# Attention's output projection as seven block products, ahead of the plain gate products

## The chip, the core and the metric

The kernel runs on one core of a Trainium2 chip. The metric is the device time of one execution in microseconds (us); three runs were timed, and one more execution was recorded by the profiler. TensorE multiplies matrices, VectorE and ScalarE do the element-wise work, GpSimd (the profile calls it POOL) does small things and issues transfers that add into their target, and SyncE (SP) issues most other transfers.

## The reference

A hybrid encoder block in float32 on 1024 tokens of width 1024: attention and a gated recurrence run on the same normalised input, each has an output projection, and two sigmoid gates merge them. An output matrix, a squared-ReLU MLP and a final norm follow. The part that the change touches:

```
u = xn @ w_in                     # q, k, v, f, i, q_hg, g_hg, gate_sb, gate_hg
o_sb = stick_breaking_attention(...)          # (1024, 512)
o_hg = hgrn2_chunkwise(...)                   # (1024, 512), normalised, times silu(g_hg)
g_a  = sigmoid(gate_sb + b[:1024])
g_b  = sigmoid(gate_hg + b[1024:])
merged = g_a * (o_sb @ w_o_sb) + g_b * (o_hg @ w_o_hg)
h = x + merged @ w_out
```

## The kernel before

**Products.** A float32 product is made of three: each operand is split into a high part, rounded to the type that TensorE takes at full rate, and the rest, the low part (hi_lo, L164: ScalarE copies the high part, VectorE subtracts it). three (L570) issues high by high, high by low and low by high. So each operand costs a ScalarE copy and a VectorE subtraction before TensorE can use it, and each tile of 512 columns by 128 rows costs three matmuls for each 128 of depth.

**Seven products for eight.** The two gates, the output matrix and the MLP are already computed in blocks of two by two with Winograd's form of Strassen's scheme: seven products of sums of blocks in place of eight. For the gates, the two halves of the input's depth and the two gate matrices are such blocks. "Plain" gate products (raw_job, L1399) need no sum of the input: for each block of 128 columns they are 36 matmuls, p1 (first half of the depth, gate a), p4 and the gate a itself. The others (products 6, 5, 7 and 3, GatePair, L1555) need sums of the normalised input (forms).

**Streams.** TensorE's order is written out by hand in two lanes: a main lane (attention's scores, turning and values, then the recurrence's levels and tails) and a filling lane of jobs. Stream (L503) holds the jobs in order. A step of a job is mostly six matmuls; advance (L558) runs some steps between two pieces of the main lane. Starting a job splits its weights, and prefetch (L525) splits the next unit's and loads the one behind. Where a manual dependency (after, L120) is given it fixes only the order of issue.

**Order around the change.** In attention, 64 items (8 heads by 8 query blocks) are filled with projections up to the plain block KT+1 (j_att); n_fill counts the steps. Then come the recurrence's heads (h = 0 to 4, a head's levels beside the tail of the one before) filled at a fixed number of steps per piece (FILL): q2, i, f3, q3, the eight plain blocks cb = 0 to 7, then the attention's projection in four jobs sb_job (L1505), each two blocks of 128 columns by two halves of the tokens by four matmul triples. The first block of an sb job multiplies by the gate from memory, the second is copied out (yd). During the sb jobs sum_forms (L1461) makes the forms of the input's sums on VectorE, from high and low parts added in place by transfers (whole_input, L1455). Last come the gates (gates, L1751): for each block x6, y5, x7, y3, with what is left of the fourth sb job in the first of them (SB_HELD).

**Weights.** out_weight_sums (L1337) builds the output matrix's sums of blocks in DRAM, by accumulating transfers from GpSimd's queue, one in every second item of attention. The gates' weight sums are made by VectorE from the loaded blocks (RawUnit.split_t, L1384, and GatePair.split, L1589).

**Memory.** On-chip tiles come from pools: 40 tiles of 1024 columns (slots), 10 of 512 (halves), two each of raw, high and low weights, 8 PSUM banks. A tile waits until an older one is free.

Of the kernel before, what the change touches and what calls it, by code (L numbers as in the profile page):

```python
# [2 lines left out]

# [36 lines left out]
def kernel(  # L40
# [404 lines left out]
    class Unit:  # L445


        late = False
# [54 lines left out]
    class Stream:  # L503
        def __init__(self, eager=False):
            self.eager = eager
            self.jobs = []
            self.pos = 0
            self.gen = None
            self.steps = 0
            self.owed_t = None  # L510
# [703 lines left out]
    def hg_tail(h):  # L1214
# [19 lines left out]
        st.finish(j_i)  # L1234
        open_block("main")
# [72 lines left out]
    a_sb, a_hg = Split("asb"), Split("ahg")  # L1308
# [38 lines left out]

    def gate_bias(which, cb):
        return prm[:, BG + which * KT + cb : BG + which * KT + cb + 1]

    def gate_cols(which, cb):
        if cb < KT:
            c0 = (C_GA, C_GB)[which] + cb * P
        else:
            c0 = C_GH + (2 * (cb - KT) + which) * P
        return slice(c0, c0 + P)

    class RawUnit(Unit):
# [5 lines left out]
        def __init__(self, cb):  # L1364
            dmas = [
                [(0, P, W_IN[:, gate_cols(w, cb)].rearrange("(k p) c -> p k c", p=P))]
                for w in range(2)
            ]
            super().__init__(f"wga{cb}", dmas)
            if cb < KT:  # L1370
                self.roomy = (1,)

        def split(self):
            if self.hl is not None:
                return
            self.load()
            ra, rb = self.raw
            h, l = (
                wpool.tile([P, 1024], F32R, tag=t, name=f"{self.name}{t}") for t in ("whi", "wlo")
            )  # L1380
            hi_lo(h, l, ra)
            self.hl = [(h, l)]

        def split_t(self, behind=None, upto=3):  # L1384
            ra, rb = self.raw
            while self.turned < upto:
                self.turned += 1
                if self.turned == 1:
                    after(sub(rb, ra, rb), behind)
                elif self.turned == 2:  # L1390
                    after(sub(rb[:, 512:], rb[:, 512:], rb[:, 0:512]), behind)
                else:
                    t = slot(f"{self.name}t", F32R)
                    self.hl.append((t[:, 0:512], t[:, 512:]))
                    after(hi_lo(*self.hl[1], rb[:, 512:]), behind)
# [3 lines left out]
    def raw_job(cb):  # L1399
        u = raw_units[cb]  # L1400

        def steps_of(ps, wt, w0, half_, k0, start):
            wh, wl = u.hl[wt]
# [8 lines left out]

        def body():
            p1, p14, g1 = (half(f"{n}_{cb}") for n in ("p1", "p14", "g1"))
            ps, p4 = bank(f"pga{cb}"), bank(f"pgq{cb}")
            if 6 <= cb < KT:
                load_g1(cb - 6)
            if 5 <= cb < KT:
                sb_units[cb - 5].load()
            if 3 <= cb < KT - 1:  # L1420
                osb[cb - 3] = slot(f"osr{cb}")
                load(osb[cb - 3], od[cb - 3])
            yield from steps_of(ps, 0, 0, 0, 0, True)
# [5 lines left out]
            yield from steps_of(p4, 1, 0, 1, 4, True)  # L1429
            add(p14, p1, p4)  # L1430
            if cb == 3 or cb == KT - 1:
                whole_input(1, int(cb == KT - 1))
            nc.gpsimd.dma_start(pd[cb][:, 1, :], p14)
            yield from steps_of(ps, 0, 4, 0, 4, False)
            if cb < KT:
                nc.scalar.activation(g1, ps, AF.Sigmoid, bias=gate_bias(0, cb))
            else:
                nc.scalar.activation(g1, ps, AF.Sigmoid)
                mul(g1, ps, g1)
            nc.scalar.dma_start(gd[cb], g1)  # L1440
            if 4 <= cb < KT:
                a_sb.put(cb - 4, osb.pop(cb - 4))
# [3 lines left out]
    side, g1r = [], {}  # L1446
# [5 lines left out]
    forms, whole = {}, {}  # L1452
    WAIT = 7

    def whole_input(i, j):  # L1455
        for kp in range(2):
            h, l = (t.bitcast(F32) for t in xn.t[i, 2 * j + kp])
            nc.gpsimd.dma_start(l, h, accum_op=ALU.add)
            whole[i, j, kp] = l

    def sum_forms():  # L1461


        raw = whole
        def split(m, kp, src):
            forms[m, kp] = tuple(slot(f"gs{n}{m}{kp}", F32R) for n in "hl")
            hi_lo(*forms[m, kp], src)

        for j in range(2):
            whole_input(0, j)  # L1470
        yield from range(WAIT)
        s1, s2 = {}, {}
        for kp in range(2):
            s1[kp] = slot(f"gs1{kp}")
            ins = add(s1[kp], raw[1, 0, kp], raw[1, 1, kp])
            if kp == 0:
                after(ins, hg_sum[0])
            yield
        for kp in range(2):
            split(5, kp, s1[kp])  # L1480
            yield
        for kp in range(2):
            s2[kp] = slot(f"gs2{kp}")
            sub(s2[kp], s1[kp], raw[0, 0, kp])
            yield
            split(6, kp, s2[kp])
            yield
        gates_in[0].load()
        gates_in[0].load_sums()
        for kp in range(2):  # L1490
            s3 = slot(f"gs3{kp}")
            sub(s3, raw[0, 0, kp], raw[1, 0, kp])
            split(7, kp, s3)
            yield
        gates_in[0].split()
        for kp in range(2):
            s4 = slot(f"gs4{kp}")
            sub(s4, raw[0, 1, kp], s2[kp])
            split(3, kp, s4)
            yield  # L1500
        gates_in[1].load()

    sb_units = []

    def sb_job(cp):  # L1505
        src = W_OSB[:, cp * 256 : (cp + 1) * 256].rearrange("(k p) c -> p k c", p=P)
        unit = Unit(f"wo0{cp}", [[(0, 256, src)]])
        unit.roomy = (0,)
        sb_units.append(unit)

        def body():
            if cp == 0:
                side.append(sum_forms())
            for j in range(2):
                cb = 2 * cp + j
                if 1 < cb + 1 < KT:
                    load_g1(cb + 1)
                g1 = g1r[cb]
                for i, cs in halves():
                    ps = bank(f"pys{cb}_{i}")  # L1520
                    for _ in proj_half(
                        ps, unit.hl[0], a_sb.mov, 4, i, lambda k: k * 256 + j * P
                    ):
                        next(side[0], None)
                        yield
                    if i == 0:
                        mul(g1, ps, g1)
                        nc.gpsimd.dma_start(yd[cb][:, i, :], g1)
                    else:
                        y = half(f"ys{cb}")  # L1530
                        nc.scalar.copy(y, ps)
                        nc.scalar.dma_start(yd[cb][:, i, :], y)

        return st.add([unit], body)
# [12 lines left out]
    j_att = raw_job(KT + 1)  # L1547
# [4 lines left out]
    j_raw = [raw_job(cb) for cb in range(KT)]  # L1552
    j_sb = [sb_job(cp) for cp in range(4)]

    class GatePair:  # L1555
# [3 lines left out]
        def load(self):  # L1559
            cb = self.cb  # L1560
            self.raw = [
                wpool.tile([P, 1024], F32, tag="raw", name=f"wg{cb}r{i}") for i in range(2)
# [26 lines left out]
        def split(self, behind=None):  # L1589
# [4 lines left out]
            after(sub(r0[:, s0], r0[:, s1], r0[:, s0]), first)  # L1594
            sub(r1[:, s0], r1[:, s1], r0[:, s0])
# [8 lines left out]
            sub(r0[:, s1], r1[:, s1], r0[:, s1])  # L1604
# [33 lines left out]
        def gated(self, which, first, second):  # L1638
# [11 lines left out]
            if which == 0:  # L1650
                muls()
# [16 lines left out]
        def x7(self):  # L1668
            self.product(7, self.X, False)
            p1, p14 = self.p[:, 0:512], self.p[:, 512:1024]  # L1670
            self.y_sum = add(p1, p1, self.Y)
            add(p1, p1, self.X)
# [15 lines left out]
        def y3(self):  # L1688
            self.product(3, self.Y, False)
            add(self.u2, self.u2, self.Y)  # L1690
# [52 lines left out]
    SB_HELD = {KT: 4}  # L1743
# [7 lines left out]
    def gates():  # L1751
        for v, n, m in zip(gates_in, gates_in[1:] + [None], gates_in[2:] + [None] * 2):
# [8 lines left out]
            st.advance(SB_HELD.get(v.cb, 0), j_sb[3])  # L1761
# [4 lines left out]
            st.finish(j_sb[3])  # L1766
# [629 lines left out]
    n_fill = 9 * (NHS - 1 + 5) + 10  # L2396
    n_first = 4
    ready = deque()
    wsums = out_weight_sums()
    done = 0  # L2400
    for i, it in enumerate(items):
# [52 lines left out]
    st.finish(j_sb[2])  # L2454
    for _ in side[0]:
# [100 lines left out]
```

## Time and profile before

| | |
|---|---|
| median of three runs | 1419.71 us (1419.6 to 1419.95) |
| the profiled execution | 1420.01 us |
| its span in the trace | 1418.2 us |
| TensorE busy | 1408.0 us, 6848 matmuls |
| VectorE busy | 1049.5 us |
| ScalarE busy | 659.3 us |
| GpSimd busy | 145.0 us |
| traffic | 241.91 MB, mean 171 GB/s |

A row of instruction groups has the source line (often a helper's), the engine, the operation, output and inputs by the program's names, how many, busy us, mean ns of one, and the idle time of the engine just ahead of them with what ended it. The chain of waits is followed back from the last instruction, at each step to what released it. The stretches give each engine's busy time between two moments, counted from the span's start.

### The profile page before, as it was taken

How to read it: one execution, taken by the hardware profiler on the slowest of the kernel's cores; microseconds unless marked ns; L12 is line 12 of the kernel's file. 1: busy time of each engine (PE TensorE's matmuls, PEld its weight loads, DVE VectorE, ACT ScalarE, POOL GpSimd, SP SyncE). 2: the span in 40 equal slices, each digit the busy share in tenths (PEclk: the TensorE clock that was granted, in tenths of full speed). 3: DMA queues.
4: the chain of work that ended last, by engine and by line, in shares of the span. 5: the costliest groups of instructions: out<-in, count | busy, mean ns of one | idle time of the engine just before them, and what ended most of it. 6: DMA issues, size and time to landing. Idle time of an engine off the chain costs nothing.

```text
span 1418.2 us, 18602 instructions
## 1 busy us (share of the span) xinstructions
PE 1408.0 (99%) x6848; PEld 1183.5 (83%) x6848; DVE 1049.5 (74%) x1429; ACT 659.3 (46%) x1127; POOL 145.0 (10%) x282
## 2 busy tenths in 40 slices
PE   9999999999999999999999999999999999999998
PEld 7888888888888888888888888888888888888886
DVE  6667777778567888887788897676766657668765
ACT  6455555554243554433244764445444443534343
POOL 3011223110011031000000300000000000000042
PEclk9999999999999999999999999999999999999999
DMA  8344445435135685364585514444446974776725
GB/s 253 83 119 127 104 101 102 104 77 154 60 75 169 224 223 186 120 214 156 162 298 194 186 53 170 163 163 142 138 145 239 351 269 148 278 274 242 273 97 186
DMA packets 169730, 241.91 MB, mean 171 GB/s; under 512 B 30844, under 2 KB 97960, under 8 KB 169640
## 3 DMA queue, kind: packets, MB, share of 16 engines
q1 hardware_dynamic: 151432, 192.48, 41.0%
q0 software_dynamic: 11616, 34.61, 9.9%
q10 hardware_dynamic: 6592, 13.63, 2.7%
q8 instruction: 54, 0.88, 0.3%
q14 instruction: 36, 0.29, 0.1%
HBM read 170.43 MB, written 68.16 MB: 168 GB/s over the span
## 4 chain that ended last, share of the span: by engine, by line
PE 97%; ACT 1%; DMA 1%; DVE 1%; issue 0%; POOL 0%; SPq 0%; POOLq 0%; DVEq 0%; ACTq 0%
PE pm L128 21%; PE pX L128 9%; PE pW L128 6%; PE pY L128 6%; PE pjqk L128 6%; PE pga L128 4%; PE gX L128 4%; PE gY L128 4%; PE pjf L128 3%; PE pjq L128 3%; PE pys L128 3%; PE pji L128 3%; PE pyh L128 3%; PE po L128 3%; PE z L128 2%; PE pwX L128 2%
## 5 line engine op out<-in xcount | busy, mean ns | idle before, releaser
L854 DVE TENSOR_TENSOR_SCAN rm<-rm,bits 128x512 f32<-128x512 f32 (+6 forms) x72 | 87.5, 1222 | 30.5 <-ACT rm L835 29.0
L156 ACT CAST whid<-w 128x1024 fp32r<-128x1024 f32 x30 | 31.6, 1054 | 153.8 <-PE pm L128 85.4
L128 PE MATMUL pm<-wlod,sh 128*128 128x512 f32 x240 | 93.6, 390 | 0.0
L128 PE MATMUL pm<-whid,sl 128*128 128x512 f32 x240 | 93.5, 389 | 0.0
L128 PE MATMUL pm<-whid,sh 128*128 128x512 f32 x240 | 93.4, 389 | 0.0
L128 PE MATMUL pm<-tl,sh 128*128 128x512 f32 (+1 forms) x210 | 81.3, 387 | 0.0
L128 PE MATMUL pm<-th,sl 128*128 128x512 f32 (+1 forms) x210 | 81.3, 387 | 0.0
L128 PE MATMUL pm<-th,sh 128*128 128x512 f32 (+1 forms) x210 | 81.3, 387 | 0.0
L161 DVE TENSOR_TENSOR wlod<-w,whid 128x1024 fp32r<-128x1024 f32 x30 | 36.7, 1222 | 55.0 <-ACT whid L156 54.8
L156 ACT CAST wTh<-pw 128x512 fp32r<-128x512 f32 (+2 forms) x96 | 43.7, 482 | 62.4 <-PE pw L131 60.8
L161 DVE TENSOR_TENSOR wTl<-pw,wTh 128x512 fp32r<-128x512 f32 (+2 forms) x96 | 50.5, 548 | 28.9 <-ACT wTh L156 28.6
L161 DVE TENSOR_TENSOR sl<-sa,sh 128x1024 fp32r<-128x1024 f32 x56 | 68.2, 1218 | 0.6 <-ACT sh L156 0.6
L2173 POOL TENSOR_SCALAR fss<-fss 128x1 f32<-128x1 f32 x8 | 4.3, 543 | 562.0 <-ACT fsc L2168 561.5
L156 ACT CAST sh<-sa 128x1024 fp32r<-128x1024 f32 x56 | 57.2, 1045 | 7.8 <-DMA sa<-ad 7.8
L128 PEld LDWEIGHTS pm<-wlod,sh 128*128 128x128 f32 x240 | 45.1, 188 | 9.9 <-DVE wlod L161 0.4
L128 PEld LDWEIGHTS pm<-whid,sh 128*128 128x128 f32 x240 | 45.0, 188 | 9.4
L128 PEld LDWEIGHTS pm<-whid,sl 128*128 128x128 f32 x240 | 45.1, 188 | 9.2
L128 PE MATMUL pX<-sqh,t1l 128*128 128x512 f32 x128 | 50.0, 390 | 0.0
L128 PE MATMUL pX<-sql,t1h 128*128 128x512 f32 x128 | 50.0, 390 | 0.0
L128 PE MATMUL pX<-sqh,t1h 128*128 128x512 f32 x128 | 49.8, 389 | 0.0
L128 PEld LDWEIGHTS pm<-th,sh 128*128 128x128 f32 x210 | 39.5, 188 | 8.1
L128 PEld LDWEIGHTS pm<-tl,sh 128*128 128x128 f32 x210 | 39.4, 188 | 8.0
(936 smaller groups left out, 4358.8 us busy)
## 6 DMA issues: line engine op xcount, KB each, us to landing
w<-in_w_ff_dram SPq DMA_DIRECT2D x72, 512.0 KB, 4.8
sa<-ad SPq DMA_DIRECT2D x52, 512.0 KB, 6.8
ad<-a SPq DMA_DIRECT2D x32, 256.0 KB, 4.5
ad<-s SPq DMA_DIRECT2D x16, 512.0 KB, 3.2
tw<-in_w_out_dram POOLq DMA_DIRECT2D x24, 256.0 KB, 5.8
pr<-pd SPq DMA_DIRECT2D x10, 512.0 KB, 5.8
x<-in_x_dram SPq DMA_DIRECT2D x8, 512.0 KB, 7.9
xnl<-xnh POOLq DMA_DIRECT2D x8, 512.0 KB, 6.2
```

Of the source, the lines that this page charges most:

```text
L128: return pe(nc.tensor.matmul(*a, **k))
L156: hi_last[0] = after(in_turn("act", nc.scalar.copy(dst, src)), hi_behind[0])
L161: nc.vector.tensor_tensor(out=dst, in0=src, in1=hi.bitcast(F32), op=ALU.subtract),
L854: sc = nc.vector.tensor_tensor_scan(out=rr, data0=rr, data1=bits[:, 1024 - nk + a : 1024 - nk + b][:, ::-1], initial=rm[:, b : b + 1] if i ...
L2173: nc.gpsimd.tensor_scalar(out=ssq, in0=ssq, scalar1=1.0 / D, scalar2=EPS, op0=ALU.mult, op1=ALU.add)
```

## The change

Five things change.

1. **The projection** is one product of 2 x 2 blocks (halves of the tokens, halves of the depth, halves of the columns) in seven products of 256 deep by 512 by 512 each, in two jobs: products 5 and 2, then 1, 6, 7, 4 and 3. Sums of the weights are made in DRAM by accumulating transfers during attention (sb_weight_sums), sums of the attention's output by VectorE (sb_sums, sb_sums_late), and partial results are kept in tiles and banks and combined as the products end.
2. **Order.** These two jobs run ahead of the eight plain blocks, which now run in the order 0, 4, 1, 5, 2, 6, 3, 7. The plain block KT+1 moves out of attention to the place behind q3, so attention has 7 steps less to fill. A plain block now multiplies its gate by the projection loaded from memory (y0). For the last four blocks the last of three products is held back and runs in the first two gates (held_job).
3. **The gates' weight sums** are of the opposite sign and come from DRAM for the plain blocks (tg4, gate_weight_sums): VectorE's two differences for each block go, and half of the second weight load.
4. **The input's sums** are made by VectorE during attention (input_sums) and stored in DRAM; sum_forms only loads and splits them. The in-place additions by transfers go.
5. **Issue order.** The forms of the projection's operands are issued behind the copy that ends a product (hi_behind), and a step of a job also advances a side list (side).

The diff, cut to its core:

```diff
@@ Stream
+                if us[-1].alone:
+                    break
...
+            next(self.side, None)
@@ hg_tail, head 0
+        if h == 0:
+            st.side = sb_sums()
@@ weight sums of the gates
+    def gate_weight_sums():
+        for op, i, c0 in (
+            (ALU.bypass, 0, C_GA), (ALU.add, 0, C_GB), (ALU.add, 1, C_GA), (ALU.add, 1, C_GB),
+        ):
+            for r in range(4):
+                rs = slice(r * P, (r + 1) * P)
+                src = W_IN[i * 512 + r * P : i * 512 + (r + 1) * P, c0 : c0 + D]
+                after(nc.gpsimd.dma_start(tg4[rs], src, accum_op=op), scored[0])
+                yield
@@ plain blocks
+    RAW_ORDER = (0, 4, 1, 5, 2, 6, 3, 7)
+    HELD = RAW_ORDER[4:]
...
+            if cb in HELD:
+                held.append((cb, last(ps, u.kept, 0)))
             else:
+                yield from last(ps, u.hl[0], 4)
@@ the input's sums
+        for kp in range(2):
...
+            s = slot(f"xs{kp}")
+            step(s, h00, h10, ALU.subtract)
+            yield
+            step(s, s, l00, ALU.add)
+            yield
+            step(s, s, l10, ALU.subtract)
+            stored(7, kp, s)
...
+            step(s, s, h11, ALU.add)
...
+            step(s4, s, h01, ALU.add)
+            yield
+            step(s4, s4, l01, ALU.add)
+            stored(3, kp, s4)
+            yield
+            step(s, s, h00, ALU.add)
+            yield
+            step(s, s, l00, ALU.add)
+            stored(5, kp, s)
@@ their forms
+            if i < 3:
+                fetch(i + 1)
+            elif i == 4:
+                while st.pos < j_raw[-1]:
+                    yield
+                for j in range(4, 8):
+                    fetch(j)
+                gates_in[1].load()
@@ the projection
+    SB_ORDER = (5, 2, 1, 6, 7, 4, 3)
...
+        def product(m, cp):
+            open_block("fill")
+            (wh, wl), (sh, sl) = sb_w[m], sb_s[m]
+            if m in (2, 5, 1, 3):
+                sb_bank[cp] = bank(f"pys{m}{cp}")
+            ps = sb_bank[cp]
+            for k in range(2):
+                c = k * 512 + cp * P
+                ks = slice(k * 512, (k + 1) * 512)
+                three(
+                    ps, wh[:, c : c + P], wl[:, c : c + P], sh[:, ks], sl[:, ks],
+                    m in (2, 5, 1, 3) and k == 0, k == 1, True,
+                )
+            return ps
...
+            for m in ms:
+                n = SB_ORDER.index(m)
+                ahead = SB_ORDER[n + 1 : n + 3]
+                for cp in range(4):
+                    end(m, cp, product(m, cp))
+                    if cp == 0 and ahead:
+                        sb_split(ahead[0])
+                        if len(ahead) > 1:
+                            sb_load(ahead[1])
+                    if cp == 0:
+                        hi_after = sb_last[0]
+                    if cp == 1 and ahead:
+                        hi_behind[0] = hi_after
+                        sb_form(ahead[0])
+                        hi_behind[0] = None
+                    if m == 2 and cp > 1:
+                        sb_sums_late((6, 3)[cp - 2])
...
@@ the jobs
-    j_att = raw_job(KT + 1)
+    j_att = j_f[2]
...
-    j_raw = [raw_job(cb) for cb in range(KT)]
-    j_sb = [sb_job(cp) for cp in range(4)]
+    raw_job(KT + 1)
+    j_sb = [sb_job(ms) for ms in ((5, 2), (1, 6, 7, 4, 3))]
+    j_raw = [raw_job(cb) for cb in RAW_ORDER]
+    j_held = held_job()
...
-    SB_HELD = {KT: 4}
+    SB_HELD = {KT: 4, KT + 1: 5}
@@ the driver
-    n_fill = 9 * (NHS - 1 + 5) + 10
+    n_fill = 9 * (NHS - 1 + 5) + 3
-        if i % 2 == 1:
+        if i % 16 != 0:
             next(wsums, None)
+        if i > 2 and i % 5 > 1:
+            next(insums, None)
...
-        upto = (j_i, j_raw[1], j_raw[6], j_sb[1], j_sb[2])[h]
+        upto = (j_i, j_sb[0], j_raw[1], j_raw[6], j_held)[h]
```

More of the change, by code (lines that the diff above doesn't have):

```diff
@@ L2 @@
 from contextlib import ExitStack
+from itertools import chain
 import concourse.bass as bass
@@ L445 @@
     class Unit:
-        late = False
+        late = alone = False
         roomy = ()
@@ L1411, in steps_of, with last @@
                     yield
+        def last(ps, hl, w0):
+            yield from steps_of(ps, hl, w0, 0, 4, False)
+            g1 = half(f"g1_{cb}")
+            if cb < KT:
+                nc.scalar.activation(g1, ps, AF.Sigmoid, bias=gate_bias(0, cb))
+                mul(g1, g1, y0.pop(cb))
+                nc.gpsimd.dma_start(yd[cb][:, 0, :], g1)
+            else:
+                nc.scalar.activation(g1, ps, AF.Sigmoid)
+                mul(g1, ps, g1)
+                nc.scalar.dma_start(gd[cb], g1)
         def body():
-            p1, p14, g1 = (half(f"{n}_{cb}") for n in ("p1", "p14", "g1"))
+            p1, p14 = (half(f"{n}_{cb}") for n in ("p1", "p14"))
             ps, p4 = bank(f"pga{cb}"), bank(f"pgq{cb}")
[L1416 to L1423, printed above, removed]
+            if cb < KT and cb not in HELD:
+                load_y0(cb)
+            if cb == HELD[0]:
+                st.side = sum_forms()
+            yield from steps_of(ps, u.hl[0], 0, 0, 0, True)
             hi_behind[0] = nc.scalar.copy(p1, ps)
@@ L1503 @@
[L1503 to L1509, printed above, removed]
-        def body():
[L1512 to L1534, printed above, removed]
+    forms = {}
@@ new lines, in sb_load, with sb_split @@
+    def sb_load(m):
+        plain = {1: (0, 0), 2: (1, 0), 3: (1, 1)}
+        sums = {5: 1, 7: 3, 6: 2, 4: 4}
+        src = sb_block(*plain[m]) if m in plain else tv[sums[m]]
+        sb_raw[m] = wpool.tile([P, 1024], F32, tag="raw", name=f"wo{m}r")
+        load(
+            sb_raw[m].rearrange("p (k c) -> p k c", k=2),
+            src.rearrange("(k p) c -> p k c", p=P),
+        )
+    def sb_split(m):
+        sb_w[m] = tuple(
+            wpool.tile([P, 1024], F32R, tag=t, name=f"wo{m}{t}") for t in ("whi", "wlo")
+        )
+        hi_lo(*sb_w[m], sb_raw.pop(m))
@@ new lines, in sb_form, with sb_sums @@
+    def sb_form(m):
+        h, l = sb_s[m] = tuple(slot(f"as{n}{m}", F32R) for n in "hl")
+        if m == 5:
+            hi_lo(h, l, sb_sum[m])
+            return
+        first, c0 = {1: (0, 0), 6: (0, 0), 7: (0, 512), 2: (2, 0), 3: (2, 0), 4: (2, 512)}[m]
+        for kk in range(2):
+            cs = slice(kk * 512, (kk + 1) * 512)
+            hi_lo(h[:, cs], l[:, cs], osb[first + kk][:, c0 : c0 + 512])
+    def sb_sums():
+        for pair in range(4):
+            osb[pair] = slot(f"osr{pair}")
+            load(osb[pair], od[pair])
+            yield
+        yield
+        l, r = (cs for _, cs in halves())
+        rows_ = [(cs, osb[kk], osb[2 + kk]) for kk, cs in halves()]
+        sb_sum[5] = slot("as5")
+        for cs, a, b in rows_:
+            sub(sb_sum[5][:, cs], a[:, r], b[:, r])
+            yield
+        for cs, a, b in rows_:
+            sub(a[:, r], a[:, l], a[:, r])
+            yield
+        sb_form(5)
+        yield
@@ L1561, in load @@
             self.raw = [
-                wpool.tile([P, 1024], F32, tag="raw", name=f"wg{cb}r{i}") for i in range(2)
+                slot(f"wg{cb}r{i}")
+                if self is gates_in[0]
+                else wpool.tile([P, 1024], F32, tag="raw", name=f"wg{cb}r{i}")
+                for i in range(2)
             ]
```

237 lines of the change are left out of this document (166 added, 71 removed).

## The prediction

> **What bounds the kernel now.** I read the page first, then the stretches of the run, then the chain of waits, and last the vector engine's own order of instructions. The page and the stretches (busy us, and behind the x the number of instructions, of TensorE, weight loads, VectorE, ScalarE, GpSimd; then granted clock, DMA share, GB/s):
>
> ```profile
> span 1418.2 us, 18602 instructions
> PE 1408.0 (99%) x6848; PEld 1183.5 (83%) x6848; DVE 1049.5 (74%) x1429; ACT 659.3 (46%) x1127; POOL 145.0 (10%) x282
> 92.00:215.00 123.00, 123.00 (x714) 106.91 (x713) 91.24 (x117) 69.38 (x159) 28.66 (x74) 1.00 0.48 112
> 215.00:322.00 107.00, 107.00 (x618) 92.86 (x618) 77.24 (x101) 62.28 (x142) 21.18 (x50) 1.00 0.48 94
> 322.00:420.00 98.00, 98.00 (x513) 83.67 (x513) 66.92 (x120) 36.34 (x78) 5.86 (x8) 1.00 0.31 91
> 420.00:477.00 57.00, 57.00 (x305) 48.52 (x304) 41.97 (x71) 25.02 (x56) 5.56 (x9) 1.00 0.64 194
> 477.00:532.00 55.00, 55.00 (x297) 46.91 (x296) 49.31 (x75) 27.31 (x56) 12.17 (x17) 1.00 0.79 216
> 555.00:577.00 22.00, 22.00 (x98) 18.21 (x97) 16.73 (x24) 8.73 (x12) 1.08 (x2) 1.00 0.60 204
> 860.00:1100.00 240.00, 240.00 (x1060) 198.81 (x1059) 165.31 (x228) 113.95 (x165) 0.00 (x0) 1.00 0.48 165
> ```
>
> TensorE is busy in every microsecond of the stretches that the change touches (attention until about 322, the recurrence with its filling until 555, the gates behind it), at full clock. A busy TensorE can still hide gaps, since one matmul is listed longer than the next one waits, so the pace must be read as well. The chain of waits (start, us, work):
>
> ```profile
> 511.99 2.77 PE pys L128 x12
> 514.76 0.89 PE sl L128 x8
> 515.65 4.10 PE pys L128 x18
> ...
> 554.93 2.75 PE gX L128 x12
> 557.68 2.72 PE gY L128 x12
> 560.40 5.44 PE pys L128 x24
> 565.84 2.72 PE gX L128 x12
> 568.56 5.44 PE pys L128 x24
> 574.00 2.72 PE gY L128 x12
> ```
>
> Piece follows piece without a gap, at 5.44/24 = 0.227 us for a 512-wide matmul, the same as 240/1060 = 0.226 where nothing but such matmuls runs. So TensorE is the bound here, and a matmul taken away is worth 0.227 us as long as no other engine comes late. The one with least left is VectorE: 49.31 of 55 us between 477 and 532.
>
> **The change, part by part.**
>
> *Matmuls.* The attention's projection is now 8 column blocks x 2 halves x 4 k x 3 = 192 matmuls (the pys of the chain). Afterwards it is 7 products x 4 column blocks x 2 k x 3 = 168, of the same 512 columns. The gate products keep their counts: 36 for each plain block, twelve of which go into the gates for four of the blocks. That is 24 fewer: 24 x 0.227 = **-5.44 us**. Moving the product KT+1 behind q3 moves its 36 matmuls (8.2 us) out of attention and changes no count.
>
> *VectorE.* What an instruction takes up is the distance of starts in a full queue, not its listed length (start, us, instruction):
>
> ```profile
> 478.04 0.68 DVE L1314 TENSOR_TENSOR p<-p,pgq 128x512 f32<-128x512 f32 x1
> 478.63 1.22 DVE L161 TENSOR_TENSOR asbl<-osr,asbh 128x1024 fp32r<-128x1024 f32 x1
> 479.77 0.68 DVE L169 TENSOR_TENSOR sl_x<-k,q 128x512 f32<-128x512 f32 x1
> ```
>
> So 0.60 us for 512 columns (listed 0.68) and 1.14 for 1024 (listed 1.22). Removed between 322 and 577: the two weight differences of eight plain blocks (8 x 1.74 = 13.9), the eight sums of the input (9.1), and of the old projection eight products with the gate, four weight and four input splits (13.9): 36.9. Added: seven weight splits (8.0), the forms (1.14 + 12 x 0.60 = 8.3), eight half sums of the attention (4.8), sixteen ends of products (9.6), eight products with the gate (4.8), and KT+1's own five steps (4.7): 40.2. In all +3.3 us in 255 us of which 193 are taken; that lies beside TensorE. What matters is where it bunches.
>
> *The tight place* is the four product groups 2, 1, 6 and 7 inside head 2 of the recurrence. Each has 4 steps of 6 matmuls (5.44 us) and needs of VectorE one weight split, two form splits, and four ends or late sums: 1.14 + 6 x 0.60 = 4.74 us. What the head itself asks for comes from the stretch 420 to 477, whose filling was plain blocks:
>
> ```profile
> 420.00:477.00 57.00, 30.20 (x120) 22.03 (x120) 0.00 (x0) 5.70 (x9) 1.00 0.64 194
> ...
> 420.00:477.00 57.00, 15.19 (x60) 10.97 (x60) 2.73 (x4) 1.00 0.64 194
> ```
>
> These are that stretch's pga and pgq alone: 180 matmuls, 30 steps or 5 blocks, each with 1.74 + 1.14 + 0.60 + 0.60 = 4.08 us of VectorE, so 20.4 of the 41.97; the head's own part is 21.6. Per four steps that is 57 x 4/30 = 7.6 us of time and 2.9 us of the head's VectorE. A new group then asks for 4.74 + 2.9 = 7.64 us in 7.6: full, not over. By listed lengths it is 1.22 + 6 x 0.68 + 2.9 = 8.2, or 0.6 us too much for each of four groups, 2.4 us. Bounds 0 to 2.4. The nearest row is a stretch where VectorE is full already, and another in attention where it nearly is:
>
> ```profile
> 97.00:112.00 15.00, 15.00 (x84) 12.83 (x83) 13.36 (x18) 8.33 (x20) 3.27 (x9) 1.00 0.56 121
> 475.00:496.00 21.00, 21.00 (x116) 18.06 (x115) 21.00 (x35) 9.08 (x16) 1.08 (x2) 1.00 0.63 200
> ```
>
> For 21 us VectorE never rests, and TensorE doesn't stop. So I take **+1.0**, below the middle.
>
> *Attention.* input_sums brings 18 vector instructions of 1024 columns, 18 x 1.14 = 20.5 us, in three of five items from the fourth on. They need 20 calls, so about 33 items, the stretch 92 to 215 (37 scans, nine for eight items):
>
> ```profile
> L854 DVE TENSOR_TENSOR_SCAN rm<-rm,bits 128x512 f32<-128x512 f32 (+6 forms) x37 | 44.5, 1213 | 9.4 <-ACT rm L835 9.3
> L161 DVE TENSOR_TENSOR wTl<-pw,wTh 128x512 fp32r<-128x512 f32 (+3 forms) x49 | 25.5, 544 | 16.9 <-ACT wTh L156 16.8
> ```
>
> VectorE has 123 - 91.24 = 31.8 us free there. The filling due (n_fill) falls from 118 to 111 steps over 64 items, so 33 items lose about 3.6 steps, some 4.2 us with the empty last step of a block left out. VectorE goes to 111.7 of 118.8 us: 94%. The new instruction is put in order behind the last low half (turn_lo), just where the engine now waits 16.8 us for ScalarE's wTh, and a scan is issued an item (3.7 us) before its transposes. Behind a late one stand this item's low half and the next scan; TensorE's values wait for them an item later. Between 0 and 20.5 us; I take **0**, since the gaps lie in the right place and the total fits.
>
> *GpSimd and the queues.* The queue gets 24 more accumulating weight transfers and eight stores of sums in attention, and loses eight in-place sums of the input later.
>
> ```profile
> L1345 POOL DMA_DIRECT2D tw<-in_w_out_dram x24 | 17.6, 764 | 0.0
> L1345 POOL DMA_DIRECT2D tw<-tw x8 | 8.5, 1302 | 0.0
> ```
>
> At most 32 x 1.3 = 42 us on an engine busy 28.66 + 21.18 of 230 us; the head's QH and QL moves and the memsets of wT stand behind them by one issue, against an item of 3.7 us. SP loses half of each second weight load and the g1 loads, and gets the eight sums (512 KB each), seven projection weights for four, and the y0 loads; DMA share is 0.48 in attention. **0**, and never below it; if the cover were gone, one issue (1.3 us) for each of a few items.
>
> *Entry of the gates.* The sums for products 7 and 3 are loaded only when the last plain block ends. x7 follows after x6, y5 and four filling steps, 2.72 + 2.72 + 5.44 = 10.9 us, as now; y3 follows at 13.6 instead of 19.0, since four steps went to KT+1.
>
> ```profile
> sa<-ad SPq DMA_DIRECT2D x52, 512.0 KB, 6.8
> hb<-hd SPq DMA_DIRECT2D x8, 512.0 KB, 9.1
> L156 ACT CAST gsh<-gs x8: 1046/1052/1072, 519.4 to 556.3; 128x1024 fp32r<-128x1024 f32 x8
> L161 DVE TENSOR_TENSOR gsl<-gs,gsh x8: 1216/1221/1226, 520.5 to 557.4; 128x1024 fp32r<-128x1024 f32 x8
> ```
>
> A load of this size takes 6.8 us, two casts 2.3: ready at 9.1, 1.8 us early. With the slow load (9.1) and VectorE full, 0.5 late, and the second and third tiles a cast later each: 0.5 + 2 x 1.2 = 2.9 us. Bounds 0 to 2.9; I take **0**, the nearer row being the 52 loads.
>
> *Sum.* The profiled execution took 1420.01 us, 1.8 more than its span: 1420.01 - 5.44 + 1.0 = 1415.6. It lay 0.3 above the median of the three runs (1419.71), so the forecast is **1415.3**.
>
> **The rivals.**
>
> *VectorE takes the saving back in the projection.* 2.4 us by listed lengths, and at each of four hand-overs one 512-wide low half not ready (0.60): 4.8 us on 1414.3, so 1419.1. For it: forms are made only two or three steps ahead, where whole units were split a job ahead. Against: the full stretch from 475 on costs nothing.
>
> *The gates wait for their sums*: 1414.3 + 2.9 = 1417.2, and with a weight split ahead of the cast (1.14) 1418.3.
>
> *Attention stretches: slower.* VectorE keeps order, and 9.3 + 16.8 = 26.1 of its 31.8 free us are waits for ScalarE. If these can't be filled, only 5.7 are free and 14.8 of the 20.5 us push TensorE: 1414.3 + 14.8 = 1429.1; with half of the 20.5 it is 1424.5. It decides from 8.3 us on (5.44 saved, 2.84 to be seen). For it: runs of three sums in a row where the queue is already nearly full (13.36 of 15 us, 97 to 112). Against: the order named above.
>
> *TensorE isn't the limit.* Weight loads fill 83%, and if the other 17% were room, 24 matmuls would fill room: 1419.7. Against: 198.81/240 is also 83% where the pace can't be had faster. The Trainium skill, Perfetto Trace Analysis, section on identifying the most-contended engine, has it that weight-load share, not matmul busy time, tells the headroom. By that rule the gain would be nothing; this trace, with 0.226 us in stretches of nothing but matmuls, shows 83% as the full pace.
>
> **How the numbers follow.** Forecast 0.62 (1413.3 to 1416.8; below the sum, since removed and neighbouring pieces run at 2.77 for 12 rather than 2.72 in places, worth up to a microsecond); VectorE in the projection 0.12; gates 0.08; attention 0.15; not the limit 0.03. This kernel's measurement can tell 0.2%, 2.84 us, from no change. Faster is 0.62, same 0.12 + 0.08 + 0.03 = 0.23, slower 0.15. The range 1413.3 to 1421.0 holds all but most of the attention case and the tail of the rest.
>
> **What would show it.** Right: 6824 TensorE instructions; the projection's pieces at 5.44 for 24, running on into the recurrence's without a gap; attention some 8 us shorter, the recurrence some 3 longer; VectorE near 94% between 92 and 211. Wrong: VectorE or ScalarE in the chain between wT and the values; sh of a projection form as what a matmul waits for; a gap ahead of KT's gX on product 7. The forecast falls if the pieces behind 92 us lose more than 2.6 us to gaps.

## The result and the profile after

The changed kernel took 1427.55 us (median of 4 runs, 1427.22 to 1428.73) against 1419.83 for the kernel before on the same chip: a ratio of 1.0056, with a 95% interval of 1.0038 to 1.0073. It is slower by 7.7 us. The forecast was 1415.3, and the range ended at 1421.0.

The profiled execution after took 1427.22 us. From its page: the span, the busy time of the engines with the number of instructions, and the shares of the chain of waits, below them the same shares of the kernel before.

```profile
span 1425.4 us, 18660 instructions
PE 1406.0 (99%) x6824; PEld 1179.2 (83%) x6824; DVE 1066.6 (75%) x1463; ACT 668.1 (47%) x1147; POOL 166.4 (12%) x318
PE 91%; DVE 4%; ACT 2%; DMA 1%; issue 1%; POOL 0%; SPq 0%; ACTq 0%; POOLq 0%; DVEq 0%
...
PE 97%; ACT 1%; DMA 1%; DVE 1%; issue 0%; POOL 0%; SPq 0%; POOLq 0%; DVEq 0%; ACTq 0%
```

The 24 matmuls are gone (6848 to 6824). Yet the span grew by 7.2 us, from 1418.2. The share of TensorE in the chain falls from 97% to 91%; VectorE's rises from 1% to 4% and ScalarE's from 1% to 2%. The stretches show where (columns as in the prediction):

```profile
92.00:215.00 123.00, 121.20 (x708) 105.07 (x708) 108.67 (x134) 69.61 (x161) 43.39 (x91) 1.00 0.77 172
215.00:314.00 99.00, 97.98 (x562) 84.51 (x561) 70.47 (x94) 56.68 (x131) 28.70 (x61) 1.00 0.81 182
...
420.00:577.00 157.00, 152.84 (x800) 128.62 (x799) 118.87 (x196) 77.44 (x165) 22.01 (x37) 1.00 0.58 190
577.00:720.00 143.00, 141.49 (x625) 116.88 (x624) 120.22 (x174) 53.18 (x69) 10.29 (x19) 1.00 0.52 175
```

The same stretches of the kernel before, three of them:

```profile
215.00:314.00 99.00, 99.00 (x573) 85.98 (x573) 71.90 (x93) 56.72 (x132) 21.18 (x50) 1.00 0.49 93
...
420.00:577.00 157.00, 157.00 (x826) 133.52 (x825) 126.41 (x193) 73.16 (x151) 24.46 (x35) 1.00 0.67 199
577.00:720.00 143.00, 143.00 (x632) 118.48 (x631) 118.36 (x169) 50.02 (x66) 9.16 (x17) 1.00 0.53 172
```

TensorE was never idle there. It now rests for 1.80, 1.02, 4.16 and 1.51 us, 8.5 us in all. A pause hidden under a matmul's listed length (0.39 us, where the next one starts after 0.227) does not show as rest. Read by the distance of starts beyond the usual one (0.227 us for 512 columns), the pauses between 95 and 725 us add up to 12.0 us: 4.8 in attention, 5.5 in the recurrence, 1.7 at the entry of the gates. Before, no single one in that stretch was above 0.14. With 5.44 saved this makes +6.6 us; the last matmul starts 5.7 us later than before (1417.2 against 1411.5 us), so the reading of the pauses is about 1 us too high.

The rest of the 7.2 us lies behind the last matmul. From its start to the end of the span it took 6.7 us before and 8.3 after; after the last output is computed, 3.5 and 5.1. At the program's end each engine has an instruction DRAIN, and GpSimd's is the one that grew. Its three, before and after (ns shortest/median/longest, first and last start in us):

```profile
L2551 POOLq DRAIN  x3: 46/102/2516, 1413.1 to 1417.9; - x3
...
L2768 POOLq DRAIN  x3: 50/93/5819, 1418.8 to 1425.1; - x3
```

The long one grew from 2.52 to 5.82 us, and in the change it ends 0.8 us before the span does. This is no pause of TensorE; the account below comes back to it.

VectorE and ScalarE don't look like the cause by their load: in the worst stretch, 420 to 577, VectorE is busy for *less* than before (118.87 against 126.41), and ScalarE for 77.44 of 157. That points to order, not load, as what stops TensorE. Three places show how. In attention, from the chain of waits after (start, us, work):

```profile
202.42 0.69 DVE wTl L162
203.11 1.13 DVE xs L1522
...
205.03 1.13 DVE xs L1522
...
207.84 0.69 DVE KS L162
...
208.55 0.68 DVE QL L162
209.23 1.13 DVE wqk7l L162
210.36 0.61 DVE wTl L162
...
211.02 1.10 PE po L129 x7
```

TensorE's values (po) wait for the low half wTl; ahead of it in VectorE's queue stand two of the new input sums (xs), two scans (rm), the head's halves KS and QL, and a weight split.

In the recurrence, from the order in time after (start, us, engine, instruction; in brackets the idle time ahead and what ended it):

```profile
515.94 0.40 PE L129 MATMUL pga<-xnh,wga1wlo 128*128 128x512 f32 x1
516.38 0.69 ACT L1460 ACTIVATE g<-pga,prm 128x512 f32<-128x512 f32 x1 [0.71 <-PE pga L129]
516.96 0.61 ACT L1097 COPY ksl<-k 128x512 f32<-128x512 f32 x1
517.62 1.05 PE L129 MATMUL sl<-q,ksl 128*128 128x128 f32 x7 [1.28 <-ACT ksl L1097]
```

The next level's matmuls (sl) need ScalarE's copy of the keys, ksl. It stands behind a sigmoid g that waits for the gate product issued just ahead. So the copy can't start before TensorE has run empty: 1.28 us.

At the entry of the gates, from the chain of waits after:

```profile
584.94 1.14 DVE ahgl L162
...
586.60 1.22 DVE wlog L162
...
588.42 1.14 DVE tgl L162
589.55 0.61 DVE pr L1324
...
590.21 1.88 PE gY L129 x7
```

Here VectorE works without a break from 576.5 us on, and gY waits for pr, which stands 13 us into this row of work.

### The profile page after: what moved, and what is told of

Its sections match the earlier page's. It is cut to its first block, busy times and chain, and to the rows that moved or that the text cites. A ratio compares the mean times of both kernels' runs of the same rounds, so it can differ in the third digit from the quotient of the medians.

```text
span 1425.4 us, 18660 instructions
## 1 busy us (share of the span) xinstructions
PE 1406.0 (99%) x6824; PEld 1179.2 (83%) x6824; DVE 1066.6 (75%) x1463; ACT 668.1 (47%) x1147; POOL 166.4 (12%) x318
## 4 chain that ended last, share of the span: by engine, by line
PE 91%; DVE 4%; ACT 2%; DMA 1%; issue 1%; POOL 0%; SPq 0%; ACTq 0%; POOLq 0%; DVEq 0%
PE pm L129 21%; PE pX L129 9%; PE pW L129 6%; PE pY L129 6%; PE pjqk L129 6%; PE gY L129 3%; PE pji L129 3%; PE pga L129 3%; PE pyh L129 3%; PE gX L129 3%; PE pjq L129 3%; PE pjf L129 3%; PE po L129 3%; PE pwX L129 2%; PE pjv L129 2%; PE z L129 2%
## 5 line engine op out<-in xcount | busy, mean ns | idle before, releaser
L157 ACT CAST wTh<-pw 128x128 fp32r<-128x128 f32 (+3 forms) x96 | 43.8, 481 | 56.3 <-PE pw L132 51.6
L129 PEld LDWEIGHTS pm<-th,sl 128*128 128x128 f32 x210 | 39.5, 188 | 8.0
```

Of the source, the lines that this page charges most:

```text
L129: return pe(nc.tensor.matmul(*a, **k))
L157: hi_last[0] = after(in_turn("act", nc.scalar.copy(dst, src)), hi_behind[0])
```

## Experiments

Two theories. **P (place):** moving KT+1 out of attention, priced at nothing in the prediction, costs most of the loss. **S (sums):** VectorE's new input sums in attention cost most, as in the third rival. The table has all runs; the time before was 1419.71 to 1419.83 in each comparison.

| kernel | median us | ratio to before, 95% |
|---|---|---|
| the change | 1427.55 | 1.0056 (1.0038 to 1.0073) |
| change, KT+1 back in attention | 1422.3 | 1.0018 (1.0009 to 1.0028) |
| change, without most input sums | 1426.11 | 1.0046 (1.0031 to 1.0061) |
| change, ksl earlier | 1422.43 | 1.0017 (1.0008 to 1.0027) |
| change, KT+1 back, ksl earlier | 1417.57 | 0.9986 (0.9976 to 0.9995) |
| the same, sums spread | 1415.93 | 0.9973 (0.9963 to 0.9983) |
| change, ksl earlier, sums spread | 1420.58 | 1.0006 (0.9997 to 1.0016) |
| change, held products' y0 earlier | 1427.48 | 1.0056 (1.0041 to 1.0071) |
| before, KT+1 moved | 1425.35 | 1.0039 (1.0024 to 1.0053) |
| before, with input sums | 1420.28 | 1.0004 (0.9995 to 1.0014) |
| before, seven steps fewer in attention | 1422.2 | 1.0018 (1.0009 to 1.0027) |
| before, ksl earlier | 1419.37 | 0.9997 (0.9987 to 1.0007) |
| before, KT+1 moved, ksl earlier | 1424.04 | 1.0033 (1.0021 to 1.0045) |

### KT+1 put back into the changed kernel

```diff
-    j_att = j_f[2]
+    j_att = raw_job(KT + 1)
...
     q_job(3)
-    raw_job(KT + 1)
...
-    n_fill = 9 * (NHS - 1 + 5) + 3
+    n_fill = 9 * (NHS - 1 + 5) + 10
```

> The changed kernel with one edit: the plain block KT+1 runs at the end of attention again, with the 7 filling steps that the old kernel had there. The changed kernel took 1427.5 us and the old one 1419.8. Theory P (moving that block is what costs: it shifts which weight cast stands in ScalarE's queue ahead of a wT cast in attention, and it puts the block's end, where ScalarE issues a store that waits for VectorE, into the recurrence): the gaps of TensorE at 223 and 269 us and those at 437 and 446 us go, about 5 us, so 1422 to 1423. Theory S (the input's sums on VectorE are what costs in attention, and the projection's own copies what costs in the recurrence): no more than 1 us better, 1426.5 to 1428.

1422.3 us: 5.2 us back. The pauses behind 200 us in attention are gone, and so is that of the gates; the one at 167 us (1.07) and 5.2 us in the recurrence stay.

### The same block moved in the old kernel

The same edit the other way round: j_att = j_f[2], raw_job(KT + 1) behind q_job(3), n_fill with + 3.

> The kernel before with one edit: the plain block KT+1 is moved out of attention to the place behind q3, and attention has 7 filling steps less. Theory P: this alone opens gaps of TensorE in attention and in the recurrence, 2 to 5 us, so 1422 to 1425. Theory S: VectorE has room in attention without the sums, and the old plain blocks follow as they did; 1419.5 to 1420.5.

1425.35 us, a little over theory P's range: the move alone costs the old kernel 5.6 us, with none of the other edits. Its pauses lie at 208, 222 and 268 us, as in the changed kernel, and in the recurrence at 515 to 523 us (2.2 and 0.9 us).

### The input's sums, taken out and put in

In the changed kernel 14 of the 18 vector instructions are left out, the loads and stores stay:

```diff
         def step(out, a, b, op):
-            after(nc.vector.tensor_tensor(out=out, in0=a, in1=b, op=op), turn_lo[0])
+            if out is not a:
+                after(nc.vector.tensor_tensor(out=out, in0=a, in1=b, op=op), turn_lo[0])
...
-            after(
-                nc.vector.scalar_tensor_tensor(
...
```

> The changed kernel, with 14 of the 18 vector instructions that form the input's sums during attention left out (what is stored is the first difference of each tile, so the sums are incomplete); stores, loads and all else stay. Theory S: the gaps of TensorE at 168 us (1.2 us) and 210 us (1.0 us), whose chain runs through these instructions, go, and some of the others in attention with them: 1424 to 1425.5. Theory P: these gaps come with the shifted filling and stay, so 1427 to 1428.

In the old kernel all 18 and their eight stores are added, their results unused:

```diff
+    insums = input_sums()
...
+        if i > 2 and i % 5 > 1:
+            next(insums, None)
```

> The kernel before with one addition: the changed kernel's 18 vector instructions for the input's sums and the eight stores of them, in the same items of attention; nothing reads what they store. Theory S: about 2.4 us of gaps between 92 and 215 us, as the changed kernel has there, so 1421.5 to 1423. Theory P: with the old filling there is room for them, 1419.5 to 1420.5.

1426.11 us, 1.4 less than the change, between the two expectations; and 1420.28, 0.6 more than before, within the measurement's uncertainty. The pause at 168 us goes without the sums, the one at 210 falls from 1.01 to 0.63; the rest stays. So the sums are a small part of the loss, and S falls as its main cause.

### Pacing alone

What does the move do in attention, where it only takes work away? In the old kernel only the number of steps due is changed; the block stays where it is and its last steps run behind the last item.

```diff
-    n_fill = 9 * (NHS - 1 + 5) + 10
+    n_fill = 9 * (NHS - 1 + 5) + 3
```

> The kernel before with one number changed: attention fills 7 steps less slowly spread over its 64 items (n_fill as in the changed kernel), and the block KT+1 stays where it was, its steps now running together after the last item. No instruction is added, removed or moved past another job. Theory P, in its sharper form (what hurts in attention is that each job's end, and with it the next weight cast, meets another item): the gaps of TensorE at 208, 222, 268 us that the moved block opened in the kernel before, 2.5 us in all, come back, 1421.5 to 1423. Against it: less filling as such does no harm, 1419.5 to 1420.5.

1422.2 us: +2.4 us, with the same pauses at 208, 222 and 268 us. From its order in time:

```profile
220.73 1.05 ACT L156 CAST wf0h<-wf0r 128x1024 fp32r<-128x1024 f32 x1 [1.85 <-PE pjqk L128]
221.69 0.75 ACT L156 CAST wTh<-pw 128x512 fp32r<-128x512 f32 x2
...
222.30 0.89 DVE L161 TENSOR_TENSOR wTl<-pw,wTh 128x512 fp32r<-128x512 f32 x2 [2.10 <-ACT wTh L156]
222.31 0.39 PE L128 MATMUL po<-wTh,V 128*128 128x256 f32 x1 [0.17 <-ACT wTh L156]
...
223.04 0.39 PE L128 MATMUL po<-wTl,V 128*128 128x256 f32 x1 [0.34 <-DVE wTl L161]
```

The next unit's weights need a buffer that the product before (pjqk) frees. Their cast (wf0h) stands in ScalarE's queue and waits 1.85 us for that product's end. Behind it stands the urgent cast wTh, and the values po wait for it and for wTl. In the kernel before, unchanged, the same casts come with no wait named:

```profile
220.78 0.57 ACT L156 CAST QH<-pjqk 64x512 fp32r<-64x512 f32 x1
221.24 1.05 ACT L156 CAST wf0h<-wf0r 128x1024 fp32r<-128x1024 f32 x1
222.19 0.47 ACT L156 CAST wTh<-pw 128x384 fp32r<-128x384 f32 x1
```

There the product had ended earlier in the item. The pauses at 208 and 268 us were not followed back in the same way. Seven steps fewer over 64 items shift the end of each job against the items, and at this hand-over the cast now comes ahead of a product's end.

### The keys' copy ahead of the sigmoid

The recurrence's pauses showed ksl behind other work of ScalarE. Here ksl is issued after the first filling step behind a level, not directly ahead of the next level's matmuls; no instruction is added.

```diff
+            if l < 6:
+                keys_due.append(lambda l=l: copy_keys(f"sl{h}_{l + 1}", 2 << l))
...
-                    st.advance(int(owed), upto)
+                    first = min(int(owed), 1)
+                    st.advance(first, upto)
+                    while keys_due:
+                        keys_due.pop()()
+                    st.advance(int(owed) - first, upto)
```

> The changed kernel with one edit in the recurrence: ScalarE's copy of the keys (ksl) for the next level is put in its queue after the first filling step behind a level, and no longer right ahead of the level's matmuls. Theory Q (in the recurrence TensorE stands because ksl waits in ScalarE's order behind a copy or sigmoid that needs the end of the product just issued, or behind a cast that nobody waits for): the gaps at 437, 446 and 515 us, 4.0 of the 5.5 us there, go: 1423 to 1424.5. Theory V (VectorE is too full there and makes the key itself late): ScalarE only waits at another place, 1426.5 to 1428.

1422.43 us: 5.1 us back, a little more than theory Q's range. From the order in time of this run, at the same level:

```profile
508.36 0.62 ACT L1103 COPY ksl<-k 128x512 f32<-128x512 f32 x1
...
513.03 1.05 PE L129 MATMUL sl<-q,ksl 128*128 128x128 f32 x8
513.23 0.69 ACT L1474 ACTIVATE g<-pga,prm 128x512 f32<-128x512 f32 x1 [0.70 <-PE pga L129]
```

The copy is done 4 us ahead of sl, and no wait stands beside sl; the sigmoid still waits for its product, but nothing urgent is behind it. The control is the same edit in the old kernel:

> The kernel before with the earlier copy of the keys alone: the control for the gain of 10 us that this edit and the block KT+1 put back brought on the changed kernel. The old kernel shows no gap of TensorE ahead of a level's matmuls, so theory Q expects nothing: 1419.3 to 1420.3. If the edit were a gain of its own, not a repair of the new order, 1414 to 1418.

1419.37 us, no difference: the old kernel's order paid nothing here. So the wait came with the new order; it wasn't there to be gained.

And in the old kernel with KT+1 moved:

> The kernel before with the block KT+1 moved (1425.4 alone) and the earlier copy of the keys. Theory Q: the gaps of 2.2 and 0.9 us ahead of a level's matmuls, which moving the block opened in the recurrence, close, and those in attention (2.6 us) stay: 1421.8 to 1422.8, what the pace alone costs (1422.2). If the moved block costs by its own vector work in the recurrence, it stays near 1425.

1424.04 us, 1.3 less than with the move alone, and a miss for theory Q, which had 1421.8 to 1422.8. The move alone, without the ksl edit, has two pauses in its recurrence, at two queues. First, from the order in time:

```profile
515.56 1.04 ACT L156 CAST wo01h<-wo01r 128x1024 fp32r<-128x1024 f32 x1 [0.46 <-PE pga L128]
516.51 0.68 ACT L1436 ACTIVATE g<-pga,prm 128x512 f32<-128x512 f32 x1
517.09 0.61 ACT L1092 COPY ksl<-k 128x512 f32<-128x512 f32 x1
...
517.75 1.16 PE L128 MATMUL sl<-q,ksl 128*128 128x128 f32 x8 [1.99 <-ACT ksl L1092]
```

This is the wait of the changed kernel: ksl stands behind a weight cast and the sigmoid. So the move alone opens it in the old kernel too, without the new projection. Then, from the chain of waits:

```profile
511.28 8.49 DMA xnl<-xnh
...
519.86 0.09 DVE gs L1314
...
521.00 1.22 DVE wo01l L161
...
523.05 0.61 DVE q L169
...
523.79 1.13 PE sl L128 x8
```

VectorE's queue is held by gs, which waits for the old kernel's in-place addition by a transfer (8.49 us); k and q of the recurrence stand behind it. The ksl edit closes the first pause (2.2 us), but TensorE then comes to the second place earlier and waits there for 2.4 us instead of 0.9. The change removes these additions, so its own recurrence doesn't have this second wait.

### Put together

> Both: the block KT+1 back in attention (1422.3 us alone) and the copy of the keys earlier. Theory Q: of the 5.2 us of gaps left in the recurrence the four ahead of a level's matmuls go, 4.0 us: 1418 to 1419, a little under the 1419.7 of the old kernel. Theory V: 1422 to 1423.

1417.57 us, a little better than theory Q's range. Then the input's sums are spread, one in every third item rather than three in a row of five:

```diff
-        if i > 2 and i % 5 > 1:
+        if i > 2 and i % 3 == 0:
             next(insums, None)
```

> As the one before, and the input's sums spread over all of attention: one vector instruction in every third item, and not three in five items of the first half. If these sums still cost there (the gap of 1.07 us at 167 us), about 1 us better than the one before; if not, the same within 0.5 us.

1415.93 us, 3.9 us under the kernel before (0.9973, 0.9963 to 0.9983), and 1.6 better than without the spreading: this version beats both. Its page and stretches:

```profile
span 1413.7 us, 18694 instructions
PE 1402.5 (99%) x6824; PEld 1179.3 (83%) x6824; DVE 1067.0 (75%) x1463; ACT 668.3 (47%) x1147; POOL 162.0 (11%) x318
```

```profile
92.00:215.00 123.00, 123.00 (x714) 106.87 (x713) 101.86 (x128) 69.39 (x159) 42.60 (x89) 1.00 0.74 160
...
420.00:577.00 157.00, 156.99 (x827) 133.69 (x826) 127.51 (x211) 82.35 (x171) 24.92 (x40) 1.00 0.60 198
577.00:720.00 143.00, 143.00 (x632) 118.25 (x631) 120.47 (x172) 51.82 (x67) 9.72 (x18) 1.00 0.54 182
```

With the same matmuls and nearly the same number of instructions in all, TensorE rests for no more than 0.01 us in these stretches. Since it doesn't stop, VectorE and ScalarE get through *more* between 420 and 577 than in the change (127.51 and 82.35 against 118.87 and 77.44), without holding it up. Last, the same with the block moved as the change has it:

> The changed kernel with the block KT+1 left where the change puts it, the earlier copy of the keys (1422.4 alone) and the input's sums spread over all of attention. The sums' share (gaps at 168 and 210 us) goes, about 1.6 us as with the block put back; the gaps of the pace (222 and 268 us), the two at 530 and 547 us and the one in the gates at 583 us stay: 1420.3 to 1421.5. The distance to the version with the block put back, 1415.9, is then what the move costs when all else is mended, about 5 us.

1420.58 us. The distance to 1415.93, 4.65 us, is the price of the move alone where all else is mended.

### The gates' pause

It was thought that gY's helper pr waits for y0, the loaded projection of a held block, so y0 was loaded at the block's start.

```diff
-            if cb < KT and cb not in HELD:
+            if cb < KT:
                 load_y0(cb)
```

> The changed kernel with one edit: the four projection halves for the held products are loaded as the blocks start, as for the other four blocks, and no longer in the gates one product ahead. If the gap of 1.67 us in the gates (588 us) comes from the load of y that the chain of waits shows ahead of it (4.8 us), 1425.5 to 1426.2. If it comes from the full vector queue behind (577 to 590 us, 13 of 13 us busy), 1427 to 1428.

1427.48 us: no effect, and the pause of 1.67 us is unchanged. The load isn't the cause. VectorE is full there, but that alone isn't the cause either, as the stretches show, two of the change and the second one again with KT+1 back:

```profile
570.00:577.00 7.00, 7.00 (x33) 5.79 (x32) 2.46 (x4) 1.02 (x2) 0.00 (x0) 1.00 0.82 234
577.00:590.00 13.00, 11.70 (x52) 9.37 (x50) 13.00 (x19) 7.26 (x9) 1.09 (x2) 1.00 0.37 137
...
577.00:590.00 13.00, 13.00 (x58) 10.60 (x57) 13.00 (x19) 6.21 (x9) 0.00 (x0) 1.00 0.30 93
```

With KT+1 back VectorE is just as full (13.00 of 13) and TensorE doesn't stop. In the change VectorE rests for 4.5 of the 7 us just ahead, and its work bunches behind. TensorE's order differs there: the held products have eight steps. With KT+1 back all eight run ahead of the first gX; in the change only one does, four run within the first gate and three within the second, right ahead of the gX and gY between which the pause lies. The moved block has six steps of the recurrence's filling, and so pushes held steps into the gates. The pause is still there with ksl earlier and with fewer sums, and gone with KT+1 back; that the held steps in the gates cause it was not tried by itself.

## Why the prediction was wrong

**The account.** From the change down, each step a run: 1427.55, KT+1 back 1422.3 (-5.2), ksl earlier 1417.57 (-4.7), sums spread 1415.93 (-1.6). The 3.9 us left under the old kernel's time are the 5.44 of the matmuls less the 1.6 us by which the program closes later: in the last version the last matmul starts 6.1 us earlier than in the kernel before (1405.4 against 1411.5 us), and the span ends only 4.5 us earlier. So the change is a gain of some 4 us under three losses, 11.6 us together, and the losses nearly add: the ksl edit is worth 5.1 or 4.7 and the spreading 1.8 or 1.6, without and with KT+1 back.

**Matmuls: right.** 24 fewer, at the pace read from the chain. That they are worth their time is borne out by the last version, where TensorE doesn't rest in the stretches above and its last matmul starts 6.1 us earlier than in the kernel before. The fourth rival, that TensorE isn't the limit, is refuted. The Trainium skill (Perfetto Trace Analysis, section on identifying the most-contended engine) judges TensorE's headroom by the weight-load share, beside the share of peak arithmetic. Read by that share alone, the 83% of weight loads would be room; the trace doesn't agree, since the share is 83% in the version that gained 3.9 us too.

**"Moving the product KT+1 ... changes no count": the step that failed.** True of the count, but the cost was then put at nothing. It is 5.2 us in the change, 5.6 in the old kernel. The prediction asked what a moved step issues, not what the steps that stay are paired with. By the pauses that go when the block goes back, the change loses 3.2 us of it in attention, 1.7 at the entry of the gates and 0.3 in the recurrence. Attention's share is mostly pacing: seven steps fewer move the end of every job there against the items, and in the old kernel that alone costs 2.4 us. The old kernel loses the other 3.2 in its recurrence: 2.2 where ksl stands behind a cast and a sigmoid, and 0.9 where VectorE is held by a transfer.

**VectorE in the projection, +1.0 (0 to 2.4): the wrong engine.** The "tight place", VectorE asked for 7.64 us in 7.6, was no bound: 127.51 of 157 us pass without a pause in the last version. The cost there is ScalarE's order, 4.7 to 5.1 us, with ScalarE half idle. The prediction had no term for ScalarE, though the change puts casts of weights and forms and the ends of products into its queue between a level and its keys. Load was counted where the place in the queue decided.

**Attention, taken 0: mis-sized, within its bounds.** The sums cost 1.4 us by leaving most of them out, and spreading them recovers 1.6 to 1.8. VectorE came to 108.67 of 123 us (88%), where 94% was forecast: the total fits, as argued, but three sums in a row of items don't. The rival "attention stretches" named the right sign and a price near the result (1424.5), yet its mechanism carries some 1.6 of the 12.3 us between forecast and result; the change is slower for other reasons.

**Gates: right that the load is hidden, wrong on the pause.** A pause of 1.67 us stood behind VectorE's queue at 588, not at the sums of products 7 and 3, and with KT+1 back it is gone.

**GpSimd, taken 0: wrong by 1.6 us, at the program's end.** No pause of TensorE that was traced names it, but the time from the last matmul to the end of the span is 6.7 us in all six traces of the old kernel and its variants, and 8.3 in all eight of the changed one. GpSimd's long DRAIN goes with the number of transfers issued from its queue: 2.5 us for 133, 3.2 for 141 (the old kernel with the sums' eight stores), 5.8 for 169. In the old kernel it ends 2.6 us before the span does, and with the eight stores 1.9, so it costs nothing there; in the change it ends 0.8 before, with nothing but closing semaphores behind it. The prediction looked at these transfers only beside the work in attention. No run takes them out of the changed kernel, so this cause is read from the traces and not tried.

The prediction's own condition, more than 2.6 us of gaps behind 92 us, was met more than four times over (12.0). With the 1.6 us at the end that is 13.6 where the sum had 1.0, so 12.6 too much; the forecast was missed by 12.3.

## What to carry to other kernels

Where one engine is busy without a gap and the others run at half load, price an edit by what stands *ahead* of each urgent instruction in the in-order queues, not by sums of busy time: a cast that waits for the very product just issued turns a half-idle engine into the bound. A step moved out of a paced stream re-pairs every later step with another piece of the main lane, so a change of pace is a change of its own, and can be tried alone (here by one number). And a change that loses may hold a gain: undone part by part, this one gave a version 3.9 us under the kernel before.

## What the runs showed that was not expected

- Seven steps fewer of 118 in attention cost 2.4 us, with no work added: a cast of 1.05 us that isn't urgent waited 1.85 us at the head of ScalarE's queue, and TensorE paused for 0.32 and 0.62 us behind it, at one hand-over of several.
- In the old kernel with the block moved, an in-place addition by a transfer (xnl from xnh) took 8.49 us on the chain of waits, and the recurrence's k and q stood behind it in VectorE's queue though they don't use its result.
- GpSimd's last DRAIN took 2.5 us with 133 transfers issued from its queue in the whole program, 3.2 with 141 and 5.8 with 169; the last of these ended behind everything but the closing semaphores, and the program's end came 1.6 us later, though GpSimd was busy for only 12% of the span.
- ScalarE, busy for 77.44 of 157 us, cost TensorE some 5 us there through the place of a copy of 0.61 us in its queue; VectorE, busy for 127.51 of 157 us in the fastest version, cost nothing.
